# One decoder layer on one core: other homes in SBUF for the tiles that the products read

## The chip, the cores and the metric

The kernel runs on 1 core of a Trainium2 chip, in one launch. The metric is the device time of a run in microseconds, from the median of several runs; lower is better. One further execution was profiled, and its trace is what the rows below come from.

## The reference

One layer of a decoder trunk for 512 tokens of width 1024, in float32. Shortened to what the kernel has to compute:

```python
h = rmsnorm(x, norm_mix)
u, q, kv, gates, mg = split(h @ w_in)                  # 1024 x 4376
a = silu(layernorm(causal_dwconv31(u1 * sigmoid(u2))))
y_conv = a @ w_conv_out                                # 512 x 1024
o = nsa_attention(q, compressed / selected / window k and v, gates, rel_bias)
y_attn = o @ w_attn_out                                # 512 x 1024
x = x + (sigmoid(mgA) * y_conv + sigmoid(mgB) * y_attn) @ w_out
g, v = split(causal_dwconv3(rmsnorm(x, norm_ffn) @ w_up))   # 1024 x 5632
x = x + (gelu(g) * v) @ w_down                         # 2816 x 1024
x = x + sigmoid(rmsnorm(x, norm_ple) @ w_ple_gate) * (p @ w_ple)
out = rmsnorm(x, norm_final)
```

## The kernel before

Every matrix product is made of three matmuls in the type float32r: each operand is split into a high part and a low part (the rest), and high x high, high x low and low x high are summed in PSUM. A helper issues the three, so that one product shows as three lines: `mm_w` (L128 to L130) for w_in, w_conv_out and w_attn_out, with the weights stationary; `mm_block` (L135 to L137) for w_up, with the weights stationary and 256 columns; `mm_a` (L141 to L143) for w_out, w_down, w_ple_gate and w_ple, where the weights are streamed and the activations are stationary. In the trace a matmul's names stand as output <- operands: `ps<-hT,whl` is w_in.

The weights come from HBM into `wraw`, are split by ScalarE (high part, L118) and VectorE (low part, L121), and lie in four slots `whl` of 8192 bytes a partition, high part first, low part 4096 bytes behind. The other operands are `hT` (w_in), `cat` (w_conv_out and w_attn_out, in hT's place), `y` (w_out) and `a` (w_down), both in eight slots of the tag "act", `hf` (w_up), `hpT` (w_ple_gate), `ppT` (w_ple), and in the attention `KQ` against `QQ` (scores, L885) and `pT` against `VV` (L830, L831). Identity transposes on TensorE (L911 and others) stand between them.

The order of all work is written out by hand. A class `Stream` holds a list of weight pieces in the order of their use, loads them on SP's queue, in order, and splits them a few pieces ahead. w_in's first part runs alone; its second part and w_conv_out fill the steps of the attention; then come w_attn_out, w_out, 22 steps of w_up with w_down in three parts between them, w_ple_gate and the last norm.

Where a tile lies follows from the order in which tags are first asked for. `cst` and `sb` are filled from below. Above `sb` lie, one after the other in time, two pools: "mixers" (hT, QQ, KQ, VV, W, acc, aT, oT and what shares their tags) and "channels" (x2, ppT, gain, second, ple, tt, hf). A tile of the second pool waits for the last readers of those tiles of the first that it overlaps.

```python
    PHASE_TAGS = (("A", "B", "VV", "W", "accX", "aT", "oT"),
                  ("x2", "hf", "ppT", "ple", "tt", "second", "gain"))
...
            self.last, self.mark = None, work("mark", (P, 1))
...
            self.rs = work("rstd", (P, 1), tag="rstd", bufs=4)
...
            nc.scalar.activation(work("warm", (P, 1)), fw(3, 0), AF.Gelu_apprx_tanh)
```

Of the kernel before, what the change touches and what calls it, by code (L numbers as in the profile page):

```python
# [12 lines left out]
AF = mybir.ActivationFunctionType  # L13
# [3 lines left out]
P = 128  # L17
# [66 lines left out]
def block_kernel(ctx: ExitStack, tc: tile.TileContext, x, p, rel_bias, norm_mix, w_in, conv_dw_w, conv_dw_b,  # L84
# [3 lines left out]
    nc = tc.nc  # L88
# [4 lines left out]
    dram = pool("dram", 1, space=bass.MemoryType.DRAM)  # L93

    PHASE_TAGS = (("A", "B", "VV", "W", "accX", "aT", "oT"),
                  ("x2", "hf", "ppT", "ple", "tt", "second", "gain"))
    phases = [tc.tile_pool(name=name, bufs=1, reuse_waits="tile") for name in ("mixers", "channels")]
    phase = [phases[0].__enter__(), None]

# [6 lines left out]
    def ps(shape=(P, 512)):  # L106
        return psum.tile(list(shape), F32, name="ps", tag="ps", bufs=8)

    def work(name, shape, dtype=F32, tag=None, bufs=1):
        tag = tag or name  # L110
        home = next((p_ for p_, tags in zip(phase, PHASE_TAGS) if tag in tags), sb)
        return home.tile(list(shape), dtype, name=name, tag=tag, bufs=bufs)
# [7 lines left out]
    def lo_of(dst, src, hi, engine=nc.vector):  # L120
        engine.tensor_tensor(dst, src, f32(hi), op=ALU.subtract)  # L121
# [33 lines left out]
    ple = {}  # L155
# [67 lines left out]
    class Stream:  # L223
# [147 lines left out]
        def done_raw(self):  # L371
            self.wholes -= 1

    st = Stream()


# [7 lines left out]
    def load_gain(g):  # L384
        gb = work("gain", (P, D), tag="gain") if phase[1] else work("gain", (P, D), tag="oT", bufs=2)
        nc.sync.dma_start(gb, bass.AP(tensor=g.tensor, offset=g.offset, ap=[[0, P], [1, D]]))
        return gb[:, 0:512], gb[:, 512:D]
# [27 lines left out]
    gain = [ps(), ps()]  # L415
    for n in range(2):
        nc.tensor.matmul(gain[n], ones, grow[:, n * 512:(n + 1) * 512], start=True, stop=True)
    warm = ps()
# [607 lines left out]
    class Pace:  # L1026
# [14 lines left out]
        def drain(self):  # L1041
            while self.live:
                self.credit = 1
                self.rate = 0
                self()
# [154 lines left out]
    x2 = work("x2", (P, NT, D))  # L1200
    ppT = work("ppT", (P, 2, 2, S), F32R)
# [95 lines left out]
    hf, hsum = {}, {}  # L1297
# [23 lines left out]
    def turn_halves(t, names):  # L1321

        src_of = dict(zip(EVERY, (*hsum[t], norms[t].h[1]))) if t >= 2 else \
            dict(zip(("a11", "a12"), norms[t].h))
        for name in names if t >= 2 else ("a11", "a12"):
            src = src_of[name]
            if name not in hf:
                hf[name] = work("hf", (P, 2, 4, 256), F32R, tag="hf", bufs=7)
            pt = ps((P, 4, P))
            for k in range(4):  # L1330
                nc.tensor.transpose(pt[:, k, :], src[:, k * P:(k + 1) * P], ident)
            ts = slice(t % 2 * P, t % 2 * P + P)
            hi_of(hf[name][:, 0, :, ts], pt)
            lo_of(hf[name][:, 1, :, ts], pt, hf[name][:, 0, :, ts])

    def fw(k, c):
        return ffnw[k // 2][:, (k % 2) * 44 + c:(k % 2) * 44 + c + 1]
# [7 lines left out]
    class Pair:  # L1345
# [61 lines left out]
        def after(self):  # L1407
# [24 lines left out]
            yield  # L1432
            lo_of(a[:, 1], o, a[:, 0])

    gain_f = load_gain(norm_ffn)
    for t in range(NT):
        p_parts(t)
# [51 lines left out]
    def step():  # L1489
        for tail in list(tails):  # L1490
            if next(tail, tails) is tails:
                tails.remove(tail)

    def slot(product, then=None, cut=True):

        product()
        if then:
            then()
        st.work()
        if cut:  # L1500
            st.pump()
        step()

    def down(f0, f1, gain, *late, **kw):
        rows_product("down%d" % f0, list(range(f0, f1)),
                     lambda k, t: (act[k][:, 0, t * P:(t + 1) * P], act[k][:, 1, t * P:(t + 1) * P]),
                     lambda t, n, o: residual(t, n, o, gain), *late, **kw)
# [5 lines left out]
    for f in range(NF):  # L1513
        this, coming = pairs[f], pairs.get(f + 1)
        if f == 0:
            slot(this.m5)
            turn_halves(3, ("s3",))
            slot(coming.m2)
            slot(this.m6)
            turn_halves(3, ("s4",))  # L1520
            slot(this.m2)
            slot(this.m7)
            turn_halves(3, ("a22",))

            nc.scalar.activation(work("warm", (P, 1)), fw(3, 0), AF.Gelu_apprx_tanh)
            slot(coming.m5)
        else:
            cut = f not in DOWN_IN
            slot(this.m6, cut=cut)
            if f > 1:  # L1530
                slot(this.m2, cut=cut and f + 1 < NF)
            else:
                step()
            if f + 1 < NF:
                coming = pairs[f + 1] = Pair(f + 1)
            if f in DOWN_IN:
                coming.b1 = st.take("11", f + 1)
                step()
                step()
                st.pump(most=1)  # L1540
                step()
                st.work()
                drain()
                down(*DOWN_IN[f], None)

            if f + 2 < NF:
                slot(coming.m1)
            else:
                step()
            slot(this.m7)  # L1550
            slot(coming.m5 if f + 2 < NF else coming.m1 if f + 1 < NF else this.m5)
        tails.append(this.after())
        slot(this.m3, coming.seed_value if 0 < f < NF - 1 else None)
        slot(this.m4, coming.seed_gate if 0 < f < NF - 1 else None)
# [91 lines left out]
```

## Time and profile before

| | |
|---|---|
| median of 3 runs | 816.78 us (816.72 to 817.11) |
| profiled execution, its own time | 817.79 us |
| its span, first to last instruction | 815.9 us |
| TensorE busy | 797.0 us (98%) |
| VectorE busy | 611.1 us (75%) |
| ScalarE busy | 442.2 us (54%) |
| GpSimd busy | 149.6 us (18%) |
| mean granted clock of TensorE, share of full speed | 0.997 |

The profiled execution's own time is about 2 us over its span; the rest lies around the first and the last instruction. Matmuls overlap in the trace: one lasts longer than the gap to the next one's start, so busy time says little of their rate, and the starts say it.

### The profile page before, as it was taken

The page shows a single profiled execution, that of the slowest core. Times are in us where ns is not written, and L with a number is a line of the kernel's source. Part 1 is how long each engine was busy: PE and PEld are TensorE (multiplying, and loading weights), DVE is VectorE, ACT ScalarE, POOL GpSimd, SP SyncE. Part 2 cuts the span into 40 slices and gives each one's busy share as a digit, 9 for nine tenths or more (in the row PEclk, how much of TensorE's full clock was granted, in tenths as well). Part 3 has the DMA queues.
Part 4 walks back from the last instruction along what each step waited for, and adds up shares of the span by engine and source line. Part 5 has one row for each costly group of instructions (what it writes and reads, how often), then busy time and mean ns, then how long its engine had stood idle before and what let it go on. Part 6 is the DMA issues. An engine that isn't in the chain of part 4 may idle for free.

```text
span 815.9 us, 12321 instructions
## 1 busy us (share of the span) xinstructions
PE 797.0 (98%) x4688; PEld 689.3 (84%) x4688; DVE 611.1 (75%) x987; ACT 442.2 (54%) x840; POOL 149.6 (18%) x181
## 2 busy tenths in 40 slices
PE   7999999999999999999999999999999999999996
PEld 6878888888888887787899997899988899888885
DVE  5469987979886887955799997369994399855564
ACT  6331523368678876333577774147762277643443
POOL 2000000000001000003365551045530255001011
PEclk9999999999999999999999999999999999999998
DMA  7256677512011112364043323413324132240412
GB/s 222 74 127 178 172 168 196 130 44 61 27 51 53 29 53 101 103 219 143 21 136 100 105 82 117 142 52 104 104 90 139 56 105 78 79 151 31 153 53 104
DMA packets 108069, 84.68 MB, mean 104 GB/s; under 512 B 4113, under 2 KB 93641, under 8 KB 108011
## 3 DMA queue, kind: packets, MB, share of 16 engines
q1 hardware_dynamic: 108010, 83.90, 35.7%
q8 instruction: 37, 0.61, 0.3%
q14 instruction: 22, 0.17, 0.1%
HBM read 79.36 MB, written 2.43 MB: 100 GB/s over the span
## 4 chain that ended last, share of the span: by engine, by line
PE 78%; DVE 13%; ACT 4%; issue 3%; DMA 1%; POOL 1%; SPq 0%; POOLq 0%; ACTq 0%; DVEq 0%
PE ps L128 9%; PE ps L130 9%; PE ps L129 9%; PE ps L142 9%; PE ps L143 9%; PE ps L141 9%; DVE whl L121 6%; PE ps L136 4%; PE ps L135 4%; PE ps L137 4%; PE ps L885 2%; PE ps L911 2%; DVE uv L1405 2%; DVE ug L1405 2%; ACT whl L118 2%
## 5 line engine op out<-in xcount | busy, mean ns | idle before, releaser
L121 DVE TENSOR_TENSOR whl<-wraw,whl 128x512 fp32r<-128x512 f32 (+1 forms) x160 | 157.9, 997 | 76.5 <-ACT whl L118 75.7
L118 ACT ACTIVATE whl<-wraw 128x512 fp32r<-128x512 f32 (+1 forms) x160 | 124.2, 797 | 101.8 <-PE ps L143 35.6
L135 PE MATMUL ps<-hf,whl 128*128 128x256 f32 x616 | 172.6, 280 | 0.7 <-ACT ps L1358 0.6
L136 PE MATMUL ps<-hf,whl 128*128 128x256 f32 x616 | 172.2, 280 | 0.2 <-DVE hf L121 0.2
L137 PE MATMUL ps<-hf,whl 128*128 128x256 f32 x616 | 172.1, 279 | 0.0
L135 PEld LDWEIGHTS ps<-hf,whl 128*128 128x128 f32 x616 | 115.8, 188 | 1.5 <-ACT ps L1358 0.8
L136 PEld LDWEIGHTS ps<-hf,whl 128*128 128x128 f32 x616 | 115.8, 188 | 0.6 <-DVE hf L121 0.4
L137 PEld LDWEIGHTS ps<-hf,whl 128*128 128x128 f32 x616 | 115.8, 188 | 0.0
L128 PE MATMUL ps<-hT,whl 128*128 128x512 f32 x256 | 102.8, 401 | 0.0
L130 PE MATMUL ps<-hT,whl 128*128 128x512 f32 x256 | 101.1, 395 | 0.3 <-DVE whl L121 0.3
L129 PE MATMUL ps<-hT,whl 128*128 128x512 f32 x256 | 101.1, 395 | 0.0
L751 DVE SCALAR_TENSOR_TENSOR acc<-aT,convw,acc 128x512 f32<-128x512 f32 x120 | 86.2, 747 | 1.0
L142 PE MATMUL ps<-whl,a 128*128 128x512 f32 x176 | 69.7, 396 | 2.7 <-DVE whl L121 2.7
L141 PE MATMUL ps<-whl,a 128*128 128x512 f32 x176 | 69.6, 396 | 0.0
L143 PE MATMUL ps<-whl,a 128*128 128x512 f32 x176 | 69.5, 395 | 0.0
L121 DVE TENSOR_TENSOR whl<-tt,whl 128x1024 fp32r<-128x1024 f32 x44 | 54.4, 1263 | 12.6 <-ACT whl L118 12.5
L319 POOL TENSOR_TENSOR tt<-wraw 128x512 f32<-128x512 f32 x44 | 60.3, 1371 | 1.2 <-DMA wraw<-in_w_up 0.8
L319 POOL TENSOR_TENSOR tt<-wraw,tt 128x512 f32<-128x512 f32 x44 | 58.6, 1332 | 3.3
L130 PEld LDWEIGHTS ps<-hT,whl 128*128 128x128 f32 x256 | 48.0, 187 | 12.3 <-DVE whl L121 0.7
L118 ACT ACTIVATE whl<-tt 128x1024 fp32r<-128x1024 f32 x44 | 46.4, 1054 | 21.2 <-PE ps L143 19.1
L128 PEld LDWEIGHTS ps<-hT,whl 128*128 128x128 f32 x256 | 48.1, 188 | 10.2 <-issue 0.2
L129 PEld LDWEIGHTS ps<-hT,whl 128*128 128x128 f32 x256 | 48.1, 188 | 9.7
(218 smaller groups left out, 1484.1 us busy)
## 6 DMA issues: line engine op xcount, KB each, us to landing
wraw<-in_w_up SPq DMA_DIRECT2D x44, 512.0 KB
wraw<-in_w_in SPq DMA_DIRECT2D x32, 512.0 KB
wraw<-in_w_down SPq DMA_DIRECT2D x20, 512.0 KB
wraw<-in_w_out SPq DMA_DIRECT2D x8, 512.0 KB
wraw<-in_w_ple_gate SPq DMA_DIRECT2D x8, 512.0 KB
W<-vdram SPq DMA_DIRECT2D x8, 264.0 KB
xin<-in_x SPq DMA_DIRECT2D x4, 512.0 KB
wraw<-in_w_ck SPq DMA_DIRECT2D x4, 512.0 KB
```

Of the source, the lines that this page charges most:

```text
L118: nc.scalar.activation(dst, src, AF.Copy, scale=scale)
L121: engine.tensor_tensor(dst, src, f32(hi), op=ALU.subtract)
L128: nc.tensor.matmul(o, hl[:, 0, j, cs], a_hi, start=start, stop=False)
L129: nc.tensor.matmul(o, hl[:, 0, j, cs], a_lo, start=False, stop=False)
L130: nc.tensor.matmul(o, hl[:, 1, j, cs], a_hi, start=False, stop=stop)
L135: nc.tensor.matmul(o, hl[:, 0, j0 + k, :], a[:, 0, k, :], start=start and k == 0, stop=False, skip_group_check=True)
L136: nc.tensor.matmul(o, hl[:, 0, j0 + k, :], a[:, 1, k, :], start=False, stop=False, skip_group_check=True)
L137: nc.tensor.matmul(o, hl[:, 1, j0 + k, :], a[:, 0, k, :], start=False, stop=k == 3, skip_group_check=True)
L141: nc.tensor.matmul(o, a_hi, w_hi, start=start, stop=False)
L142: nc.tensor.matmul(o, a_hi, w_lo, start=False, stop=False)
L143: nc.tensor.matmul(o, a_lo, w_hi, start=False, stop=stop)
L319: sub = lambda to, x_, y_: nc.gpsimd.tensor_tensor(to, x_, y_, op=ALU.subtract)
```

## The change

Three edits. The tag `rstd` (four slots of 32 bytes) is asked for before the stream is made, so its slots lie at the bottom of `sb` and not behind pT; everything between moves up by 128 bytes. The `warm` tile, which an activation writes only to have a table loaded, takes a slot of `rstd` in place of its own 32 bytes at the top of `sb`, so the pool above begins 32 bytes lower. A new tile `apart` of 32 bytes, never written, stands in the second pool behind ppT, so that what follows it there stays where it was.

```diff
     PHASE_TAGS = (("A", "B", "VV", "W", "accX", "aT", "oT"),
-                  ("x2", "hf", "ppT", "ple", "tt", "second", "gain"))
+                  ("x2", "hf", "ppT", "ple", "tt", "second", "gain", "apart"))
...
+    work("rstd", (P, 1), tag="rstd", bufs=4)
     st = Stream()
...
+    work("apart", (P, 8))
     gain_f = load_gain(norm_ffn)
...
-            nc.scalar.activation(work("warm", (P, 1)), fw(3, 0), AF.Gelu_apprx_tanh)
+            nc.scalar.activation(work("warm", (P, 1), tag="rstd", bufs=4), fw(3, 0), AF.Gelu_apprx_tanh)
```

The homes in the two built programs, as the first byte in a partition:

| tiles | before | after |
|---|---|---|
| rstd, four slots from | 64416 | 6784 |
| act (X, mg, S, y, a), eight slots from | 6816 | 6944 |
| wraw, two slots from | 39584 | 39712 |
| pT, two slots from | 56224 | 56352 |
| whl, four slots from | 64544 | 64544 |
| QQ, later x2 | 114496 | 114464 |
| KQ, later ppT | 130880 | 130848 |
| hT, later cat | 147264 | 147232 |
| VV | 180032 | 180000 |
| gain | 139072 | 139072 |
| second, two slots | 143168, 147264 | 143168, 147264 |
| hf and hpT, seven slots from | 171840 | 171840 |

The parts, slots and blocks inside these tiles that a matmul reads begin at multiples of 256 bytes from the tile's first byte. So a distance modulo 256 between two operands holds for a whole product:

| streamed against stationary | before | after |
|---|---|---|
| hT or cat against whl (w_in, w_conv_out, w_attn_out) | 32 | 0 |
| whl against y or a (w_out, w_down), either way round | 128 | 0 |
| whl against ppT (w_ple) | 224 | 0 |
| pT against VV | 96 | 0 |
| hf against whl (w_up) | 32 | 32 |
| whl against hpT (w_ple_gate) | 224 | 224 |
| KQ against QQ | 0 | 0 |

On TensorE, VectorE and GpSimd the same instructions stand in the same order with the same waits. On SP's queue one wait moves. The rows are its loads between w_out and the second block of w_up, with the semaphores that each waits for; `wraw_3469` and `wraw_3520` are the two slots of the tag "second" before, `wraw_3471` and `wraw_3522` after:

```order
L299 DMA wraw_3438<-in_w_out 128x2x512 [waits DMAHW2_49,DVE_49]
L299 DMA wraw_3467<-in_w_up 128x8x128 [waits DMAHW5_49,DMAHW3_49,DVE_49]
L299 DMA wraw_3469<-in_w_up 128x8x128 [waits DMAHW6_49]
L299 DMA wraw_3518<-in_w_up 128x8x128 [waits DMAHW7_49,DMAHW4_49,DVE_49]
L299 DMA wraw_3520<-in_w_up 128x8x128 [waits DMAHW0_49,PE_49]
L299 DMA ple_3522<-in_w_ple 128x2x512 [waits DMAHW1_49]
```

After the change:

```order
L299 DMA wraw_3440<-in_w_out 128x2x512 [waits DMAHW2_49,DVE_49]
L299 DMA wraw_3469<-in_w_up 128x8x128 [waits DMAHW5_49,DMAHW3_49,DVE_49]
L299 DMA wraw_3471<-in_w_up 128x8x128 [waits DMAHW6_49,PE_49]
L299 DMA wraw_3520<-in_w_up 128x8x128 [waits DMAHW7_49,DMAHW4_49,DVE_49]
L299 DMA wraw_3522<-in_w_up 128x8x128 [waits DMAHW0_49]
L299 DMA ple_3524<-in_w_ple 128x2x512 [waits DMAHW1_49]
```

The wait for TensorE (PE_49, for the last product that reads cat) stands at the first slot's load in place of the second's, two loads earlier; no load changes its place.

On ScalarE the place is the first step of w_up, around the activation that loads a table; the names are tiles with their numbers, and the rows are those of before:

```order
L1391 ACTIVATE ps_3344<-ps_3346 128x256 [waits PE_49,Activation_49]
L118 ACTIVATE hf_3712<-ps_3951 128x4x128 [waits PE_49]
L1525 ACT_TABLE_LOAD
L1525 ACTIVATE warm_3958<-ffnw1_824 128x1
L1376 ACTIVATE m5_3973<-ps_3960 128x256 [waits PE_49]
```

And of after:

```order
L1392 ACTIVATE ps_3345<-ps_3347 128x256 [waits PE_49,Activation_49]
L118 ACTIVATE hf_3714<-ps_3953 128x4x128 [waits PE_49]
L1527 ACT_TABLE_LOAD
L1527 ACTIVATE warm_3960<-ffnw1_825 128x1
L1377 ACTIVATE m5_3975<-ps_3962 128x256 [waits PE_49]
```

The activation keeps its place and has no wait in either, though it now writes a slot that a norm's factor held before.

## Rows read from the trace of the kernel before

**Rows 1.** The page's busy times: us, share of the span, instructions.

```profile
PE 797.0 (98%) x4688; PEld 689.3 (84%) x4688; DVE 611.1 (75%) x987; ACT 442.2 (54%) x840; POOL 149.6 (18%) x181
```

**Rows 2.** Waits of TensorE: us in total, times, longest us.

```profile
PE ps L142 <- DVE whl L121: 2.7, 2, 1.3
```

**Rows 3.** TensorE's groups by shape: line, names, shapes, count, busy us, mean ns, idle.

```profile
L135 PE MATMUL ps<-hf,whl 128*128 128x256 f32 x616 | 172.6, 280 | 0.7 <-ACT ps L1358 0.6
...
L128 PE MATMUL ps<-hT,whl 128*128 128x512 f32 x256 | 102.8, 401 | 0.0
...
L141 PE MATMUL ps<-whl,a 128*128 128x512 f32 x176 | 69.6, 396 | 0.0
...
L128 PE MATMUL ps<-cat,whl 128*128 128x512 f32 x64 | 26.1, 408 | 0.0
L141 PE MATMUL ps<-whl,y 128*128 128x512 f32 x64 | 25.6, 400 | 0.0
```

**Rows 4.** TensorE's timeline (start us, duration us): w_in, w_up, w_ple_gate.

```profile
53.68 0.39 PE L128 MATMUL ps<-hT,whl 128*128 128x512 f32 x1
...
81.68 0.39 PE L128 MATMUL ps<-hT,whl 128*128 128x512 f32 x1
...
451.94 0.28 PE L135 MATMUL ps<-hf,whl 128*128 128x256 f32 x1
...
484.84 0.28 PE L135 MATMUL ps<-hf,whl 128*128 128x256 f32 x1
...
764.22 0.40 PE L141 MATMUL ps<-whl,hpT 128*128 128x512 f32 x1
...
799.92 0.40 PE L141 MATMUL ps<-whl,hpT 128*128 128x512 f32 x1
```

**Rows 5.** The same timeline: w_up around 486, two thirds of w_down.

```profile
486.12 0.38 PE L137 MATMUL ps<-hf,whl 128*128 128x256 f32 x1
486.34 0.28 PE L135 MATMUL ps<-hf,whl 128*128 128x256 f32 x1
...
493.41 0.28 PE L135 MATMUL ps<-hf,whl 128*128 128x256 f32 x1
...
501.65 0.39 PE L141 MATMUL ps<-whl,a 128*128 128x512 f32 x1
...
502.35 0.40 PE L141 MATMUL ps<-whl,a 128*128 128x512 f32 x1
502.59 0.40 PE L142 MATMUL ps<-whl,a 128*128 128x512 f32 x1
...
534.42 0.39 PE L141 MATMUL ps<-whl,a 128*128 128x512 f32 x1
...
617.24 0.40 PE L141 MATMUL ps<-whl,a 128*128 128x512 f32 x1
...
643.84 0.40 PE L141 MATMUL ps<-whl,a 128*128 128x512 f32 x1
```

**Rows 6.** The same timeline in the attention: scores, and w_in behind transposes.

```profile
192.30 1.17 PE L885 MATMUL ps<-KQ,QQ 128*128 128x512 f32 x4
193.31 0.40 PE L128 MATMUL ps<-hT,whl 128*128 128x512 f32 x1
...
203.37 0.47 PE L128 MATMUL ps<-hT,whl 128*128 128x512 f32 x1
203.68 0.39 PE L129 MATMUL ps<-hT,whl 128*128 128x512 f32 x1
...
204.37 0.39 PE L129 MATMUL ps<-hT,whl 128*128 128x512 f32 x1
```

**Rows 7.** Timeline of TensorE (cat's last reader) and of SP's queue.

```profile
350.15 0.39 PE L130 MATMUL ps<-cat,whl 128*128 128x512 f32 x1
...
370.64 7.93 SPq L299 DMA_DIRECT2D wraw<-in_w_up  x4
```

## Prediction

> **What bounds the kernel now.** I read the page's busy times first, then the waits of TensorE, then TensorE's groups by shape, and last its timeline, for the distance from one start to the next. The page says that TensorE is the bound nearly everywhere: 797.0 of 815.9 us [rows 1]. The largest entry in the list of its waits is 2.7 us in two waits, the longer 1.3 us [rows 2]. So a change that moves no instruction of TensorE changes the time if it changes how fast matmuls follow each other, or if it lengthens a wait, and otherwise it doesn't.
>
> A busy time of a matmul (393 to 408 ns) overlaps with the next one; what counts is the gap between two starts. The counts stand with the groups by shape (each line stands for one of three that a product's helper issues): 768 matmuls of 512 columns for w_in (3 x 256), 192 for w_conv_out and w_attn_out together (3 x 64), 192 for w_out, 528 for w_down, and 1848 of 256 columns for w_up (3 x 616) [rows 3].
>
> The gaps, each from a first and a last row and the number of starts between them [rows 4]: w_in 81.68 - 53.68 = 28.00 us for 120 matmuls, 233.3 ns. w_up 484.84 - 451.94 = 32.90 us for 282, 116.7 ns, half of it for half the columns. w_ple_gate 799.92 - 764.22 = 35.70 us for 153, 233.3 ns. Three kinds of operand, three ranges of addresses, and the same 0.4557 ns per column.
>
> There is a second cadence [rows 5]. The first third of w_down: 534.42 - 501.65 = 32.77 us for 141 matmuls, 232.4 ns. Its second third: 643.84 - 617.24 = 26.60 us for 114, 233.3 ns. And w_up, once a matmul at 486.12 was followed only 0.22 us later: 493.41 - 486.34 = 7.07 us for 60, 117.8 ns, where it had been 116.7 ns until then. So either product can run in either cadence at unchanged homes; in w_up what came between the two was one late start. I call them the even cadence (233.3 and 116.7) and the loose one (232.4 and 117.8).
>
> **The change part by part.** The orders of TensorE, VectorE, ScalarE and GpSimd hold the same instructions, shapes and waits as before; what differs is where tiles lie, and one wait of the DMA queue on SP.
>
> *The homes.* By the table above, what a product streams and the stationary parts that are loaded beside it now lie a multiple of 256 bytes apart for w_in, w_conv_out, w_attn_out, w_out, w_down, w_ple and the attention's pT products. Before, these distances were 32, 128 or 96 bytes modulo 256. For w_up and w_ple_gate they stay at 32. Does that distance set the gap? The trace of before holds several distances already:
> - 32 (w_in, w_up) and its reverse, 224 (w_ple_gate streams whl): 233.3, twice 116.7, 233.3 [rows 4].
> - 128 (w_down): 232.4 in one third and 233.3 in the next [rows 5].
> - 0, the distance of after: the attention's scores, KQ streamed against QQ. Four such matmuls of 512 columns took from 192.30 to 193.31, 1.01 us [rows 6]. Four of w_in behind the same kind of transposes took from 203.37 to 204.37, 1.00 us [rows 6]. The difference is no more than the rounding of the rows.
>
> So the distance that the change introduces was in the kernel already, at the ordinary gap. I take 0 ns per matmul. The evidence is thin in one way: four matmuls in a row, at a distance that is also 0 modulo 512, where after has 256. Some 1808 matmuls move (768 + 192 + 192 + 528, 48 of w_ple and 80 pT products counted from the program), so 1 ns on each is 1.8 us. Bounds from rows: the fastest run of three inside a dense stretch is 204.37 - 203.68 = 0.69 us, 230 ns [rows 6], which on all would be -3.3 x 1808 = -6.0 us. The slowest single gap is 502.59 - 502.35 = 0.24 us [rows 5], which would be +6.7 x 1808 = +12.1 us. Both belong to single places in a pattern whose mean is 232 to 233, hence zero as the value taken.
>
> The Trainium skill bears on this from two sides. "TensorE: Matmul & The Clock Gate", Part 2, says that TensorE has two independent read ports on SBUF, and that loading the next weights doesn't take bandwidth from the matmul that streams; by that the distance between the two can't matter, and the sum is 0. The trace agrees as far as the rows with distance 0 go. The same page, under "Back-to-back issue gap", gives N / 2.4 + 2.5 ns, 216 ns for 512 columns, where the rows show 233.3 at a granted clock of 0.997 of full speed: here the measurement differs, by 17 ns, and if it was the operands' homes that cost these 17 ns, the change would be worth up to an estimated 31 us by that page.
>
> *The wait on SP.* Two loads of w_up go to the slots of "second", at 143168 and 147264. With cat at 147232, cat's first 32 bytes now lie in the first slot, so the wait for cat's last reader stands two loads earlier in the queue. That reader starts at 350.15 [rows 7]; the four loads of w_up start to issue at 370.64, behind three of w_out that wait for VectorE [rows 7]. The wait is over 20 us before its load is at the head of the queue, so it costs nothing. Were that cover gone, the loads behind it (the second pair of w_up and w_ple) would be late, and VectorE's and GpSimd's work on them next.
>
> *The warm tile.* The activation that only loads a table now writes to a slot of rstd. It gets no wait and keeps its place, so 0. The tile "apart" is never written; it only keeps the second phase's tiles where they were.
>
> *Alignment.* Every home moves by 32 or 128 bytes. hT lay at 0 modulo 64 and now lies at 32, but whl as the streamed operand lies at 32 too, and goes at 233.3 in w_ple_gate [rows 4]. So 0.
>
> **The sum.** 0 + 0 + 0. The profiled execution has a span of 815.9 and took 817.79; the runs shown have a median of 816.78, 1.0 below it. I forecast 816.8 for the median, 816.0 to 817.6 for the case itself. The measurement of this kernel can tell from no change about 0.2%, 1.6 us.
>
> **The rivals.**
> 1. *The loose cadence in the moved products.* The gap depends on the operands after all, a little, or a wait ends at another moment, and the products of 512 columns that now run evenly (1808 less the 352 of w_down's first and last third) go at 232.4: -0.93 x 1456 = -1.4 us, 815.4. For it: w_down did both. Against: w_in ran evenly over 120 matmuls [rows 4].
> 2. *The loose cadence in w_up (slower).* Place: w_up's products, behind their wait of 0.6 us on ScalarE [rows 3]. If a late start there leaves the loose cadence, 1848 matmuls pay 1.1 ns each: +2.1 us, 818.9. It decides when a stretch of w_up shows 117.8; rows 5 show that one late start is enough, and the kernel before ran evenly in most of w_up. Nothing that the change moves touches w_up's distances, so it must come from the timing of what stands ahead.
> 3. *The distance sets the gap, in the change's favour.* By the 230 ns of rows 6, 810.8. The page's 216 ns would go further than any row, as told above. Against: 32, 128, 224 and 0 all read 232 to 233.
> 4. *The distance sets the gap, to its harm.* Streaming and weight load meet in the same place of SBUF at every step: at 240 ns, 828.9. Against: the scores at distance 0.
> 5. *The earlier wait holds the loads of w_up.* It would need cat's last reader 20 us later; under 0.01.
>
> **How the numbers follow.** No change 0.58; rival 1, 0.14; rival 2, 0.10; rival 3, 0.11; rival 4, 0.07. Half of rival 1 falls within 0.2% (815.15 is the edge). Faster by over 0.2%: 0.11 + 0.07 = 0.18. Slower by over 0.2%: 0.10 + 0.07 = 0.17. Within: 0.65. The range leaves out rivals 3 and 4, 0.18 together: from 815.4 less the longest wait that could fall away, 1.3, to 818.9 plus another ScalarE wait of w_up, 0.6: 814.1 to 819.5.
>
> **What would show it.** Right: the dense stretches of w_in, w_out, w_attn_out and w_down again at 232 to 233.5 ns, w_up at 116.7, the same waits of TensorE, and the four loads of w_up issued at about 370 us. Wrong in its main step: a mean gap of w_in, over a hundred matmuls, under 232 or over 234.5. Rival 2 is seen in w_up alone, with w_in unchanged. If the gaps are all as before and the time isn't, a wait has grown, and the waits of TensorE name it.

## The result and the profile after

The changed kernel takes 808.8 us, the median of 4 runs (808.35 to 809.55), where the kernel before on the same chip took 816.94 us (816.72 to 817.27). The ratio is 0.990, with a 95% interval of 0.9888 to 0.9912: about 1% faster, and outside the range that was forecast. The profiled execution took 808.57 us, with a span of 806.5 us and a granted clock of 0.997, as before.

The page's busy times of the changed kernel, which answer to [rows 1]:

```profile
PE 787.4 (98%) x4688; PEld 688.2 (85%) x4688; DVE 610.7 (76%) x987; ACT 442.1 (55%) x840; POOL 149.5 (19%) x181
```

And the head of the waits of TensorE (us in total, times, longest us), which answer to [rows 2]:

```profile
PE ps L142 <- DVE whl L121: 2.7, 2, 1.3
PE ps L418 <- DMA grow<-in_norm_mix: 2.3, 1, 2.3
PE ps L1332 <- DVE hhalf L459: 1.4, 2, 1.1
```

The largest wait for weights is the same as before, and the other engines' busy times differ by 0.4 us at most. TensorE alone is busy 9.6 us less, with the same 4688 matmuls. So the matmuls follow each other faster. The timeline of TensorE says where; the columns are start and duration in us. There are 180 matmuls between the two rows of w_in, 126 between those of w_out, 531 in w_up, 156 in w_down and 156 in w_ple_gate:

```profile
44.40 0.39 PE L129 MATMUL ps<-hT,whl 128*128 128x512 f32 x1
...
85.20 0.39 PE L129 MATMUL ps<-hT,whl 128*128 128x512 f32 x1
...
348.20 0.39 PE L142 MATMUL ps<-whl,y 128*128 128x512 f32 x1
...
376.76 0.39 PE L142 MATMUL ps<-whl,y 128*128 128x512 f32 x1
...
418.00 0.28 PE L137 MATMUL ps<-hf,whl 128*128 128x256 f32 x1
...
479.95 0.38 PE L137 MATMUL ps<-hf,whl 128*128 128x256 f32 x1
...
492.38 0.39 PE L143 MATMUL ps<-whl,a 128*128 128x512 f32 x1
...
527.74 0.39 PE L143 MATMUL ps<-whl,a 128*128 128x512 f32 x1
...
755.84 0.40 PE L142 MATMUL ps<-whl,hpT 128*128 128x512 f32 x1
...
792.24 0.40 PE L142 MATMUL ps<-whl,hpT 128*128 128x512 f32 x1
```

The gap from start to start is 40.80 / 180 = 226.7 ns in w_in, 28.56 / 126 = 226.7 in w_out and 35.36 / 156 = 226.7 in w_down: a third cadence, which no row of before shows, 6.7 ns below the even one [rows 4] and 5.7 below the loose one [rows 5]. w_up stays at 61.95 / 531 = 116.7 ns and w_ple_gate at 36.40 / 156 = 233.3, as before [rows 4]. The products whose distance went to 0 modulo 256 have the new cadence; the two whose distance stayed don't.

The starts of the stages in the two timelines, and how far the lead grows in each stage:

| stage | begins before | begins after | gained in it |
|---|---|---|---|
| head, up to w_in's first product | 0 | 0 | 0.95 |
| w_in alone (504 matmuls) | 30.90 | 29.95 | 2.78 |
| attention, with the rest of w_in and half of the 192 that read cat | 166.87 | 163.14 | 1.02 |
| the other half of those | 326.56 | 321.81 | 0.59 |
| w_out and w_ple's first half, to w_up | 351.17 | 345.83 | 1.04 |
| w_up, first stretch | 407.38 | 401.00 | -0.17 |
| w_down, first third | 494.47 | 488.26 | 0.93 |
| w_up, second stretch | 535.11 | 527.97 | -0.07 |
| w_down, second third | 603.73 | 596.66 | 1.09 |
| w_up, third stretch | 644.54 | 636.38 | 0.01 |
| w_down, last third | 709.12 | 700.95 | 1.14 |
| w_ple_gate and w_ple's second half | 762.74 | 753.43 | 0.02 |

Together 9.3 us between the two executions. The 0.95 us of the head is no part of the gain: in experiment 2, where all tiles read up to there have the changed kernel's homes, w_in begins at 30.93. What is left, 8.4 us, agrees with the 8.1 between the medians.

### The profile page after: what moved, and what is told of

The parts are those of the page before. It is cut to its first block, busy times and chain, and to the rows that moved or that the text cites. A ratio compares the mean times of both kernels' runs of the same rounds, so it can differ in the third digit from the quotient of the medians.

```text
span 806.5 us, 12321 instructions
## 1 busy us (share of the span) xinstructions
PE 787.4 (98%) x4688; PEld 688.2 (85%) x4688; DVE 610.7 (76%) x987; ACT 442.1 (55%) x840; POOL 149.5 (19%) x181
## 4 chain that ended last, share of the span: by engine, by line
PE 82%; DVE 11%; issue 3%; ACT 3%; DMA 1%; POOL 1%; SPq 0%; POOLq 0%; ACTq 0%; DVEq 0%
PE ps L128 9%; PE ps L130 9%; PE ps L129 9%; PE ps L142 9%; PE ps L143 9%; PE ps L141 9%; PE ps L136 5%; PE ps L135 5%; PE ps L137 5%; DVE whl L121 5%; PE ps L886 2%; PE ps L912 2%; PE ps L692 2%; PE ps L831 2%; PE ps L832 1%
## 5 line engine op out<-in xcount | busy, mean ns | idle before, releaser
L121 DVE TENSOR_TENSOR whl<-wraw,whl 128x512 fp32r<-128x512 f32 (+1 forms) x160 | 158.1, 999 | 75.6 <-ACT whl L118 74.9
L128 PE MATMUL ps<-hT,whl 128*128 128x512 f32 x256 | 101.8, 398 | 0.0
L130 PE MATMUL ps<-hT,whl 128*128 128x512 f32 x256 | 100.0, 391 | 0.3 <-DVE whl L121 0.3
L129 PE MATMUL ps<-hT,whl 128*128 128x512 f32 x256 | 100.0, 391 | 0.0
L142 PE MATMUL ps<-whl,a 128*128 128x512 f32 x176 | 68.7, 390 | 2.7 <-DVE whl L121 2.7
L141 PE MATMUL ps<-whl,a 128*128 128x512 f32 x176 | 68.7, 390 | 0.0
L143 PE MATMUL ps<-whl,a 128*128 128x512 f32 x176 | 68.5, 389 | 0.0
L121 DVE TENSOR_TENSOR whl<-tt,whl 128x1024 fp32r<-128x1024 f32 x44 | 54.4, 1265 | 12.4 <-ACT whl L118 12.3
```

What stands on the lines that cost most here:

```text
L128: nc.tensor.matmul(o, hl[:, 0, j, cs], a_hi, start=start, stop=False)
L129: nc.tensor.matmul(o, hl[:, 0, j, cs], a_lo, start=False, stop=False)
L130: nc.tensor.matmul(o, hl[:, 1, j, cs], a_hi, start=False, stop=stop)
L141: nc.tensor.matmul(o, a_hi, w_hi, start=start, stop=False)
L142: nc.tensor.matmul(o, a_hi, w_lo, start=False, stop=False)
L143: nc.tensor.matmul(o, a_lo, w_hi, start=False, stop=stop)
```

## Experiments

Theory A: the distance between what a matmul streams and the stationary parts, taken modulo 256 bytes, sets the cadence, for each product by itself. The rivals are named in the expectations; each stands before its run. The kernel before, run beside each on the same chip, took 816.3 to 817.8 us (median).

**1. The mixer products' homes alone, and the tag act's alone.** The three edits can be split, since hT, cat and ppT lie above `whl` and move with the warm tile, while y and a lie below and move with `rstd`. The first kernel drops the early `rstd`, the second drops the other two edits:

```diff
-    work("rstd", (P, 1), tag="rstd", bufs=4)
     st = Stream()
```

```diff
-    work("apart", (P, 8))
...
-            nc.scalar.activation(work("warm", (P, 1), tag="rstd", bufs=4), fw(3, 0), AF.Gelu_apprx_tanh)
+            nc.scalar.activation(work("warm", (P, 1)), fw(3, 0), AF.Gelu_apprx_tanh)
```

> Only the first pool is moved down by 32 bytes (hT and cat at distance 0 from whl; y and a stay at 128). Theory A, the distance modulo 256 sets the gap: w_in, w_conv_out, w_attn_out and w_ple at 226.7 ns in long stretches, w_out and w_down at 232 to 233.5 as before; the time falls by the 5.3 us that the changed kernel had gained by the end of w_attn_out, to about 811.5 (810.8 to 812.5). Rival B, the gap is a state that TensorE falls into once, early, and keeps, whatever the distance: then either all products of 512 columns show 226.7 and the time is that of the changed kernel, 808.8, or none does and it is 816.9.

> Only the early slots of rstd: the eight act slots move up by 128 bytes (y and a at distance 0 from whl), hT and cat stay at 32. Theory A: w_out and w_down at 226.7 ns, w_in, w_conv_out and w_attn_out at 233.3; the time falls by what the changed kernel gained in w_out (0.9) and the three parts of w_down (0.9, 1.1 and 1.1), to about 812.9 (812.3 to 813.8). Rival B: all at 226.7 and 808.8, or none and 816.9.

Measured: 813.22 us for the mixers alone (ratio 0.9946, 0.9933 to 0.9959), 813.39 us for act alone (0.9949, 0.9936 to 0.9962). The timeline of the first kernel, w_in and then w_down's first third:

```profile
44.20 0.39 PE L129 MATMUL ps<-hT,whl 128*128 128x512 f32 x1
...
85.00 0.39 PE L129 MATMUL ps<-hT,whl 128*128 128x512 f32 x1
...
493.07 0.40 PE L143 MATMUL ps<-whl,a 128*128 128x512 f32 x1
...
529.47 0.39 PE L143 MATMUL ps<-whl,a 128*128 128x512 f32 x1
```

And the same places in the second:

```profile
44.95 0.39 PE L129 MATMUL ps<-hT,whl 128*128 128x512 f32 x1
...
86.95 0.39 PE L129 MATMUL ps<-hT,whl 128*128 128x512 f32 x1
...
497.25 0.39 PE L143 MATMUL ps<-whl,a 128*128 128x512 f32 x1
...
532.61 0.39 PE L143 MATMUL ps<-whl,a 128*128 128x512 f32 x1
```

180 matmuls of w_in take 40.80 us in the one (226.7 ns) and 42.00 in the other (233.3); 156 of w_down take 36.40 (233.3) and 35.36 (226.7). Each product follows its own distance, and none takes over the cadence of a product before it: rival B is out. The first kernel's time misses its range (810.8 to 812.5). The 5.3 us of its forecast held the 0.95 of the head; without them 4.4 us were to be expected, and 817.78 - 813.22 = 4.6 were measured. The two gains, 0.54% and 0.51%, add up to the whole change's 1.0%. In the second kernel w_up ran in the loose cadence for most of its first stretch (117.8 ns over 600 matmuls from 422.71 us), at an unchanged distance of 32: that is the prediction's second rival.

**2. Also w_up's and w_ple_gate's operands at distance 0.** The changed kernel without the tile that holds them in place:

```diff
-    work("apart", (P, 8))
     gain_f = load_gain(norm_ffn)
```

> The changed kernel without the tile apart, so that hf (w_up, 256 columns) and hpT (w_ple_gate) lie at distance 0 from whl too. Theory A taken to the end: w_ple_gate at 226.7 ns (-1.1 us), and w_up at 113.3, half of 226.7, in place of 116.7 (-6.2 us for 1848 matmuls): about 801.5 (800.5 to 803). If the gain belongs to 512 columns alone, w_up stays at 116.7 and the time is about 807.7. Rival D, at 256 columns a distance of 0 harms, as the weight load fills the whole gap: w_up above 117.8, and the time over 810.

Measured: 809.66 us (0.9901, 0.9887 to 0.9915), a span of 808.0. The timeline, 600 matmuls of w_up and 156 of w_ple_gate:

```profile
418.88 0.28 PE L137 MATMUL ps<-hf,whl 128*128 128x256 f32 x1
...
490.88 0.28 PE L137 MATMUL ps<-hf,whl 128*128 128x256 f32 x1
...
758.30 0.39 PE L142 MATMUL ps<-whl,hpT 128*128 128x512 f32 x1
...
793.66 0.39 PE L142 MATMUL ps<-whl,hpT 128*128 128x512 f32 x1
```

w_ple_gate takes the short cadence, 226.7 ns, as theory A has it. w_up takes 120.0 ns, which is slower than at 32, the cadence of rival D: **for matmuls of 256 columns distance 0 is not the good one.** It costs little of what it seems to, and the time stays just under the 810 that rival D gave. w_up's stretches together became 4.6 us longer, but w_down's first two parts became 2.9 us shorter, since TensorE's longest wait of the changed kernel, 2.7 us for w_down's weights, is gone; the waits of this run begin so:

```profile
PE ps L418 <- DMA grow<-in_norm_mix: 2.4, 1, 2.4
PE ps L467 <- ACT hrow L546: 1.4, 1, 1.4
PE ps L1332 <- DVE hhalf L459: 1.4, 2, 1.0
```

So the wait for the weights that VectorE splits (DVE whl L121), which fell away, made up for a part of what w_up lost. That a faster w_up would for the same reason be worth less than its matmuls say is argued from this, not shown.

**3. Distance 0 modulo 512, and w_up at 64.** A pad of 256 bytes ahead of hT, another tag asked for early (32 bytes for each of 8 slots, so act moves by 256), and `apart` of 64 bytes:

```diff
+    work("ss", (P, 3), tag="ss", bufs=8)
...
+    work("between", (P, 64))
     hT = work("hT", (P, 2, KC, S), F32R, tag="A", bufs=1)
...
-    work("apart", (P, 8))
+    work("apart", (P, 16))
```

> The changed kernel with hT and cat 256 bytes higher and the act slots 256 bytes higher, so that both lie at 0 modulo 512 from whl, where the changed kernel has 256 modulo 512; hf and hpT at 64 modulo 256. If only the distance modulo 256 counts, the products of 512 columns keep 226.7 ns and the time stays at 808.8 (808 to 809.6). If 512 counts, they are at 232 to 233.5 and the time is 816 to 818. w_up and w_ple_gate at distance 64 are a look at another distance: 116.7 and 233.3 if 64 is like 32.

Measured: 809.14 us (0.9897, 0.9883 to 0.9911). The timeline of w_in, 180 matmuls in 40.80 us:

```profile
44.54 0.39 PE L129 MATMUL ps<-hT,whl 128*128 128x512 f32 x1
...
85.34 0.39 PE L129 MATMUL ps<-hT,whl 128*128 128x512 f32 x1
```

w_in again takes 226.7 ns: 256 and 0 modulo 512 do alike, so what counts is the distance modulo 256. w_up's 600 matmuls from 418.09 to 488.75 us went at 117.8 ns, so 64 is not like 32 for them; w_ple_gate, at 192, stayed at 233.3.

**4. All addresses 64 bytes higher, all distances kept.** Until here every matmul operand of the good products also began 32 bytes above a multiple of 256.

```diff
+    work("low", (P, 16))
     work("rstd", (P, 1), tag="rstd", bufs=4)
```

> The changed kernel with an unread tile of 64 bytes ahead of all work tiles: every operand and every weight part starts 64 bytes higher, and no distance between them changes. Theory A (the distance between the streamed operand and the weights' part, taken mod 256 bytes, sets the gap of two matmuls): 226.67 ns in w_in, w_conv_out, w_attn_out, w_out, w_down and w_ple as in the changed kernel, 116.67 ns in w_up, and 808.8 us in all (808.3 to 809.6). Rival C (the address of a tile itself matters, and the operands were moved onto a good one, 32 above a multiple of 256): 233.3 ns everywhere, and about 816.9 us.

Measured: 808.63 us (0.9899, 0.9882 to 0.9915). The timeline of w_in, 180 matmuls in 40.80 us:

```profile
44.34 0.39 PE L129 MATMUL ps<-hT,whl 128*128 128x512 f32 x1
...
85.14 0.39 PE L129 MATMUL ps<-hT,whl 128*128 128x512 f32 x1
```

Rival C is out: the distance counts, and the address itself doesn't, as far as one shift by 64 bytes can tell.

**5. A ladder of distances for w_up.** The seven buffers of `hf` are made 8224 bytes instead of 8192, so that each stands 32 further; the room comes from one small table (peT) that is moved into the pool of the first phase:

```diff
-                hf[name] = work("hf", (P, 2, 4, 256), F32R, tag="hf", bufs=7)
+                hf[name] = work("hf", (P, 2056), F32R, tag="hf", bufs=7)[:, 0:2048].rearrange(
+                    "p (a k c) -> p a k c", a=2, k=4)
```

> The changed kernel with each of the seven buffers of w_up's operand 32 bytes further from its neighbour than 8192, so that they stand 32, 64, 96, 128, 160, 192 and 224 bytes (mod 256) from the weights' parts in one run (room for it comes from one small table that is given a home which is free again later; the buffers of w_ple_gate's operand share the same homes, four of them). Theory A with only distance 0 special: the buffer at 32 shows 116.67 ns for a matmul of 256 columns, the one at 64 117.79 ns as in the run with 64 bytes, and the rest lie between 116.67 and 120.0; w_ple_gate stays at 233.3 ns in all four homes; about 809 us. Rival E (some other distance gives 256 columns the shorter cadence, half of 226.67, so 113.3 ns): one of the seven shows 113 to 114 ns, and the products that read it are 3% shorter.

Measured: 809.09 us in the one run. w_up reads each buffer for 12 matmuls, then goes to the next. The timeline holds the first matmul that reads the buffer at 96, then those for 64, 160 and 224:

```profile
434.05 0.28 PE L135 MATMUL ps<-hf,whl 128*128 128x256 f32 x1
...
435.48 0.28 PE L135 MATMUL ps<-hf,whl 128*128 128x256 f32 x1
...
436.84 0.28 PE L135 MATMUL ps<-hf,whl 128*128 128x256 f32 x1
...
438.25 0.28 PE L135 MATMUL ps<-hf,whl 128*128 128x256 f32 x1
```

12 matmuls take 1.43 us at 96, 1.36 at 64 (113.3 ns a matmul) and 1.41 at 160. In 19 of 22 visits the buffer at 64 went at 113.3 ns, half of 226.7, and in the other three at 117.8, the cadence of the whole kernel at 64 in experiment 3. So neither expectation holds: another distance than 0 can give the short cadence, but the same distance gives two. w_ple_gate, at 32, 96 and 224 here, stayed at 233 (its fourth buffer, at 64, is read by six matmuls of 512 columns at a time, too few to tell).

**6. w_ple_gate at 0 and w_up left at 32.** Buffers of 8448 bytes (33 x 256) keep all seven at one distance; `hf` stands at their start, `hpT` 224 bytes in. The room comes from three small tables (w2k, w2v, peT) that are moved into the pool of the first phase.

```diff
-    hpT = [work("hpT", (P, 2, KC, P), F32R, tag="hf", bufs=7) for t in range(NT)]
+    hpT = [work("hpT", (P, 2112), F32R, tag="hf", bufs=7)[:, 56:2104].rearrange(
+        "p (a k c) -> p a k c", a=2, k=KC) for t in range(NT)]
```

> The changed kernel with w_ple_gate's operand at distance 0 as well, and w_up's operand left at 32: the buffers that the two share are 8448 instead of 8192 bytes, w_up's operand stands at their start and w_ple_gate's 224 bytes into them (three small tables of the attention phase get a home that is free again later, which makes the room). Theory A (distance mod 256 sets the cadence of each product by itself): w_up 116.67 ns as in the changed kernel, w_ple_gate 226.67 ns; the stretch of w_ple_gate was 1.1 us shorter in the run in which its operand stood at 0, so 807.7 us (807.0 to 808.4). Rival: w_ple_gate is cut by its waits and not by its cadence, and nothing changes, 808.8.

Measured: 807.56 us (0.9878, 0.9864 to 0.9893), 1.2 us under the changed kernel's median, 807.7 expected. The intervals of the two ratios overlap a little, so the place in the trace has to bear it out, 156 matmuls of w_ple_gate in 35.36 us:

```profile
755.86 0.39 PE L142 MATMUL ps<-whl,hpT 128*128 128x512 f32 x1
...
791.22 0.39 PE L142 MATMUL ps<-whl,hpT 128*128 128x512 f32 x1
```

That is 226.7 ns, against 233.3 in the changed kernel, and the stage takes 43.8 us from its first matmul to the last of the kernel instead of 44.8. This is the fastest kernel of the study.

**7. What gives w_up its short cadence?** Four kernels like that of experiment 6, with only the places inside `hf`'s buffers changed; in the first, s4's buffer alone stands at 96 and the other six at 64:

```diff
+                at = {'s4': 16}.get(name, 8)
+                hf[name] = work("hf", (P, 2112), F32R, tag="hf", bufs=7)[:, at:at + 2048].rearrange(
```

> As the run with w_ple_gate's operand at 0, but w_up's operand stands at 64 in six of its seven buffers and at 96 in the seventh (s4), the one read just ahead of a22's. In the ladder the products that read the buffer at 64, right behind the one at 96, showed 113.33 ns, where a whole kernel at 64 showed 117.67. Theory F (256 columns have more than one steady cadence at one distance, and a step of the distance just ahead decides which; it then stays while the distance stays): six of seven products at 113.3 to 114, the seventh at 118 to 119, mean 114.3, w_up's some 1850 matmuls 4.3 us shorter; between none and all of it reaches the end, since w_down waits longer for its weights if w_up ends sooner: 803.4 to 807.7. Rival G (the short cadence is only a passage of a dozen matmuls): a22's products at 113.3, the five behind them back at 117.7, mean 117.3, and about 808.5 us.

Measured: 808.2 us (0.9886, 0.9870 to 0.9903). Of the 22 stretches behind s4, 21 went at 117.8 ns, a22's own products too (the other, of mean 114.9 without its waits, changed on the way), so both theories miss. The other three kernels, with s1 (192), then s3 (128) as well, and then the ladder with one buffer held:

> Only s1 at 192 and s4 at 96, the other five buffers at 64. If two steps are enough and the cadence is kept: a22, s2, a12, a11 and s3 at 113.3 to 114, s1 near 116, s4 near 118.9, mean 114.6, 3.8 us less in w_up and 804 to 807.6 us. If not: 117.7 in the five, about 808.2 us as in the run with one step.

> Only the three buffers ahead of a22 stand as in the ladder (s3 128, s1 192, s4 96), the other four at 64. If three steps of history are enough and the cadence is kept: s1 at 116, s4 at 118.9, a22, s2, a12 and a11 at 113.3 to 114, s3 at 118.4, mean 115.3, 1.2% below 116.67 for some 1850 matmuls, 2.5 us less in w_up and 805 to 807.6 us. Rival G: a22 alone is short, mean 117.2, about 808.3 us.

> w_up's buffers at the ladder's distances in the order in which they are read (a11 32, s3 128, s1 192, s4 96, a22 64), but s2, which is read behind a22, stays at 64 instead of 160; a12 at 224; w_ple_gate at 0. Theory F, amended (the short cadence at 64 needs all of the history that the ladder gave it, and is then kept): a22's twelve matmuls at 113.3 to 114 as in the ladder, and s2's twelve at 113.3 too. Rival G (a passage that ends by itself): a22 at 113.3 to 114, s2 back at 117.7. If a22 is at 117.7 here, the distance of the buffer is not what the ladder showed. Time within 1 us of 807.6 in either case.

Measured, in one run each: 808.06, 808.38 and 808.1 us. With two, three and five of the seven buffers at other distances, 8, 11 and 19 of the 22 stretches behind s4 had a median gap under 114.5 ns, most of them a mean of 113.3 to 113.5; nearly all the others went at 117.8. Two of those with three steps, one after the other in the timeline, each from its first matmul to the first behind its 48:

```profile
425.88 0.28 PE L135 MATMUL ps<-hf,whl 128*128 128x256 f32 x1
...
431.32 0.28 PE L135 MATMUL ps<-hf,whl 128*128 128x256 f32 x1
...
435.60 0.28 PE L135 MATMUL ps<-hf,whl 128*128 128x256 f32 x1
...
441.25 0.28 PE L135 MATMUL ps<-hf,whl 128*128 128x256 f32 x1
```

The first 48 take 5.44 us, 113.3 ns each, the next 48 take 5.65, 117.7, at the same distance from the same buffers. So the cadence is as a rule held while the distance stays (the passage of rival G is out: 48 matmuls in a row kept it). It can turn at a break: in the same kernel 21 matmuls from 474.90 us went at 113.3 ns, one at 477.53 was followed only 0.22 us later, and 23 from 477.75 went at 117.8, at the same distance; rows 5 show the like in the kernel before. What ahead of a stretch, or at a break, decides between the two stays open, and none of these kernels reached the times that a kept short cadence was to give (803.4 to 807.7 us): the mean gap of w_up was 116.5 ns with three steps, against 116.7.

**8. The prediction's evidence, tried.** Only KQ is moved, to 32 bytes from QQ modulo 256; a pad of 192 bytes keeps hT at 0.

```diff
+    work("between", (P, 48))
     hT = work("hT", (P, 2, KC, S), F32R, tag="A", bufs=1)
...
-    KQ = work("KQ", (P, 2, 2, NG, S), F32R, tag="B", bufs=2)
+    KQ = work("KQ", (P, 4104), F32R, tag="B", bufs=2)[:, :4096].rearrange("p (a b g s) -> p a b g s", a=2, b=2, g=NG)
```

> The changed kernel with KQ moved to 32 bytes (mod 256) from QQ, everything else at the changed kernel's distances. It tries the evidence on which the prediction rested. If four scores behind transposes are too few to show a cadence: the four scores that took from 188.19 to 189.21 in the changed kernel take 1.01 to 1.02 us here too, although their distance is now 32. If four do show the distance's cadence: 0.91 us in the one kernel and 1.01 in the other cannot both be, and this run would have to be slower than the changed kernel's 1.02 by a tenth. Besides: where scores stand in pairs between six matmuls of w_in, w_in's should no longer settle at 226.67 ns, some 37 ns more for each such group of eight, about 0.5 us more in all: 809.3 us.

Measured: 808.0 us in the one run. Its timeline in the attention: scores in pairs between six matmuls of w_in, and later four scores behind transposes:

```profile
166.41 0.63 PE L887 MATMUL ps<-KQ,QQ 128*128 128x512 f32 x2
166.88 0.39 PE L128 MATMUL ps<-hT,whl 128*128 128x512 f32 x1
...
168.25 0.63 PE L887 MATMUL ps<-KQ,QQ 128*128 128x512 f32 x2
...
187.92 1.18 PE L887 MATMUL ps<-KQ,QQ 128*128 128x512 f32 x4
188.94 0.39 PE L128 MATMUL ps<-hT,whl 128*128 128x512 f32 x1
```

The same places in the changed kernel, where the scores' distance is 0:

```profile
166.90 0.62 PE L886 MATMUL ps<-KQ,QQ 128*128 128x512 f32 x2
167.35 0.39 PE L128 MATMUL ps<-hT,whl 128*128 128x512 f32 x1
...
168.71 0.62 PE L886 MATMUL ps<-KQ,QQ 128*128 128x512 f32 x2
...
188.19 1.18 PE L886 MATMUL ps<-KQ,QQ 128*128 128x512 f32 x4
189.21 0.39 PE L128 MATMUL ps<-hT,whl 128*128 128x512 f32 x1
...
190.60 0.39 PE L831 MATMUL ps<-pT,VV 128*128 128x512 f32 x1
```

Four scores behind transposes take 1.02 us at distance 32 and 1.02 us at distance 0: they say nothing of the distance. The group of two scores and six matmuls of w_in, with no transposes in it, does: 1.81 us for eight (226 ns) where both distances are 0, 1.84 where the scores are at 32. The half microsecond that this was to cost doesn't show in the time; ten or so groups make 0.3 us, less than one run's scatter.

## Why the prediction was wrong, point by point

**The step that failed** is "I take 0 ns per matmul", and in it the reading of four scores at distance 0 as the ordinary gap. In its place the runs show -6.7 ns: a settled gap of 226.7 ns at distance 0, against 233.3 at 32. The rows were right: 1.01 us for four. But a cadence settles only some way behind a break. In the changed kernel the six matmuls of w_in behind the four scores still take 1.39 us (189.21 to 190.60), some 231 ns each, though all of them stand at 0; where nothing but products stands in a row, six take 1.36 (167.35 to 168.71), 227. Experiment 8 shows the four blind to their distance. The prediction called this evidence "thin in one way", four in a row, and then went by it; the other doubt that it named, 0 modulo 512 against 256, is settled by experiment 3 and was none.

**The size.** Had the step been taken at -6.7 ns for all 1808 moved matmuls, the sum would have been -12.1 us. Measured between the executions are -8.4. w_in alone gave 2.78 of 504 x 6.7 = 3.4 us (419 of its 504 gaps are at 226 or 227 ns, the others lie at or just behind a break), and w_down 3.16 of some 3.2 (its first and last third ran in the loose cadence before, which leaves 5.7 for 352 of the 528). The attention gave 1.02 us for its 360 matmuls of w_in, w_conv_out and w_attn_out, which would be 2.4: transposes break the rows every eight matmuls or so, and only a third of these gaps lie at 226 to 228 ns.

**The bounds.** -6.0 us "on all" was made from the fastest three, 230 ns, which stand just behind transposes and so show a passage too; the true cadence lay below any mean of three in those rows. The prediction's own working held a figure on the other side of it, from the Trainium skill's "TensorE: Matmul & The Clock Gate", "Back-to-back issue gap": 216 ns for 512 columns (the section calls it the gap of an isolated matmul), with the remark that the homes might be what costs the difference. They cost 6.7 of the 17 ns; the other 10.7 stay at every distance that was run. Part 2 of the same page of the Trainium skill, with two read ports that don't depend on each other, was cited for a sum of 0; whatever the ports do, experiments 1 to 4 show that the gap does depend on how far the two operands are from each other, modulo 256 bytes.

**The rivals.** The third, the distance in the change's favour, is what happened, at 0.11, and 2 us beyond the 810.8 that it was given. Its counter-argument, "32, 128, 224 and 0 all read 232 to 233", is true of the first three and false of the last. Rival 2 did not come in the changed kernel (w_up 116.7 ns) but did in the second of experiment 1. Rival 1 and rival 4 are out: no moved product is at 232.4 or above where it runs undisturbed. Two distances in the prediction's text slip, without weight on its sum: w_ple stood at 224 before, and w_ple_gate stays at 224, as the table has them.

**The other steps held.** The wait on SP: cat's last reader starts at 344.81, and the four loads of w_up issue from 364.85, again 20 us later and again behind w_out's:

```profile
351.02 8.75 SPq L299 DMA_DIRECT2D wraw<-in_w_out  x3
364.85 7.77 SPq L299 DMA_DIRECT2D wraw<-in_w_up  x4
```

The warm tile and the alignment cost nothing that any stage shows, and experiment 4 moves every address by 64 bytes at no change. The forecast's test was the right one and named its own failure: "a mean gap of w_in, over a hundred matmuls, under 232".

## What to carry to other kernels

Where TensorE is the bound, take the mean gap from start to start of each product over a hundred matmuls, and set it beside the distance modulo 256 bytes between what the product streams and its stationary parts: here 0 was worth 3% on float32r matmuls of 512 columns, and the same 0 cost 3% on those of 256, so each shape wants its own run. A layout is changed in a few bytes of padding, and a pad for one tile moves all tiles behind it, so count the distances of all products before and after. And evidence for a rate has to be longer than the time that the rate takes to settle: a few matmuls behind transposes show a transition, and a kernel in which only those few differ can tell.

## What the runs showed of the hardware

- The settled gap of float32r matmuls at a granted clock of 0.997, by distance modulo 256 between streamed and stationary operand. 512 columns: 226.7 ns at 0; 233.3 at 32 and 224; 232.4 to 233.3 at 128; 233 at 192 (experiment 3) and 96 (experiment 5). 256 columns: 120.0 at 0 (experiment 2), 116.7 (at times 117.8) at 32, 117.8 or 113.3 at 64 (experiments 3, 5 and 7).
- Some 3 to 11 matmuls pass behind a break until the 226.7 is reached: 3 at w_out's start in the changed kernel (from 345.83 us), 11 at the start of w_down's last third (from 700.95).
- At 256 columns and a distance of 64 two cadences, 113.3 and 117.8 ns, each kept as a rule for a whole stretch, of 600 matmuls for the longer (experiment 3) and up to 60 for the shorter; a late start can turn the one into the other, and what else decides is open. 113.3 in all of w_up would be an estimated 1848 x 3.4 = 6 us less for its matmuls, and no layout here reached it.
- Why the distance matters is not shown by any run: none looks inside the reads.
